# Row softmax: stores issued by Pool, DVE and ACT as loops over tiles

## The chip, the cores and the metric

The kernel runs on one core of a Trainium2 chip. The metric is the device time of one execution in microseconds (us). A core has several engines that run their own instruction streams: DVE (the vector engine), ACT (the scalar engine), POOL (GpSimd), PE (the matrix engine, unused here for arithmetic) and SP (which only issues transfers and waits). All transfers between HBM (the chip's memory) and SBUF (the core's working memory of 128 partitions) are carried out by 16 DMA engines, whichever engine issues them.

## The reference

A softmax over the last axis of a float32 array of 32 x 512 x 1024, with the input divided by a temperature of 0.5:

```
scaled = x / temperature
shifted = scaled - np.max(scaled, axis=-1, keepdims=True)
exp_x = np.exp(shifted)
return (exp_x / np.sum(exp_x, axis=-1, keepdims=True)).astype(np.float32)
```

There are 16,384 rows of 1,024 elements. 67.11 MB are read and 67.11 MB written.

## The kernel before, in words

The rows are cut into 16 tiles. A tile is 128 partitions x 8 rows x 1,024 elements, 4 MB; each partition holds eight neighbouring rows, so that its part of a tile is one piece of 32 KB in HBM and in SBUF. Six tile buffers (`BUFS = 6`) go round. All work is done in place in the tile.

A tile is worked on in two groups of four rows (`GROUP = 4`). The order is written out by hand, one step per group, and the program is fully unrolled: `maximum(g)` (DVE: the maxima of four rows in one `tensor_reduce`, L70, and the bias, which is minus twice the maximum, L73), `exponential(g)` (ACT: four activations of one row each, L79, which also sum up the row into `sums`), then `divide(g - 1)` (DVE: `reciprocal`, L91, and four multiplications of one row each by its reciprocal, L93) and `store(g - 1)`. DVE thus takes the maxima of the next group, which may lie in the next tile, before it divides the last one.

Loads are issued by SP (L61): six at the start, and then one each time a store has been issued. As a buffer is used anew, that load waits on SP until the store of the tile six before it has landed. Stores are issued by ACT (L101), one for a whole tile of 4 MB, after its second group has been divided; ACT waits for this division at that place in its own stream. `top`, `bias`, `sums` and `recip` are small buffers that go round in fours. The waits between the engines are set by the framework from what each instruction reads and writes.

Of the kernel before, what the change touches and what calls it, by code (L numbers as in the profile page):

```python
# [1 line left out]

# [4 lines left out]

TILES = [[8]] * 16  # L10
BUFS = 6

GROUP = 4


@with_exitstack
def kernel(
    ctx: ExitStack,
    tc: tile.TileContext,
    x: bass.AP,  # L20
    temperature: bass.AP,
    out: bass.AP,
):
    nc = tc.nc
    f32 = mybir.dt.float32
    scale = 1.0 / float(temperature)
    extreme = mybir.AluOpType.max if scale > 0 else mybir.AluOpType.min

    P = 128
    xf = x.flatten_outer_dims()  # L30
    of = out.flatten_outer_dims()
    n, d = xf.shape
    assert sum(sum(ks) for ks in TILES) * P == n

    data = ctx.enter_context(tc.tile_pool(name="data", bufs=BUFS))
    stats = ctx.enter_context(tc.tile_pool(name="stats", bufs=4))


    groups, first, r = [], [], 0
    for i, ks in enumerate(TILES):  # L40
        first.append(r)
        r += sum(ks)
        a = 0
        for k in ks:
            for b in range(0, k, GROUP):
                m = min(GROUP, k - b)
                groups.append((i, a + b, m, (a, k) if b + m == k else None))
            a += k

    def dram(t, i):  # L50
        k = sum(TILES[i])
        block = t[P * first[i] : P * (first[i] + k), :]
        return block.rearrange("(p k) d -> p k d", p=P, k=k)

    tiles, small = [], []

    def load():
        i = len(tiles)
        if i < len(TILES):
            xt = data.tile([P, sum(TILES[i]), d], f32, name="xt")  # L60
            nc.sync.dma_start(out=xt, in_=dram(xf, i))  # L61
            tiles.append(xt)

    def maximum(g):
        i, a, k, _ = groups[g]
        top, bias, sums, recip = (
            stats.tile([P, k], f32, name=name) for name in ("top", "bias", "sums", "recip")
        )
        small.append((bias, sums, recip))
        nc.vector.tensor_reduce(  # L70
            out=top, in_=tiles[i][:, a : a + k, :], axis=mybir.AxisListType.X, op=extreme
        )
        nc.vector.tensor_scalar_mul(bias, in0=top, scalar1=-scale)  # L73

    def exponential(g):
        i, a, k, _ = groups[g]
        bias, sums, _ = small[g]
        for b in range(k):
            nc.scalar.activation(  # L79
                tiles[i][:, a + b, :],  # L80
                tiles[i][:, a + b, :],
                mybir.ActivationFunctionType.Exp,
                bias=bias[:, b : b + 1],
                scale=scale,
                accum_out=sums[:, b : b + 1],
            )

    def divide(g):
        i, a, k, _ = groups[g]
        _, sums, recip = small[g]  # L90
        nc.vector.reciprocal(recip, sums)  # L91
        for b in range(k):
            nc.vector.tensor_scalar_mul(  # L93
                tiles[i][:, a + b, :], in0=tiles[i][:, a + b, :], scalar1=recip[:, b : b + 1]
            )

    def store(g):
        i, _, _, part = groups[g]
        if part:
            a, k = part  # L100
            nc.scalar.dma_start(out=dram(of, i)[:, a : a + k, :], in_=tiles[i][:, a : a + k, :])  # L101
            if a + k == sum(TILES[i]):
                load()

    with tc.manual_schedule():
        for _ in range(BUFS):
            load()
        for g in range(len(groups) + 1):  # L110
            if g < len(groups):
                maximum(g)
                exponential(g)
            if g > 0:
                divide(g - 1)
                store(g - 1)


# [1 line left out]
_INS = ['x', 'temperature']  # L120
_OUTS = [((32, 512, 1024), 'float32')]

_NUMBERS = {'temperature': 0.5}


# [26 lines left out]
```

## Time and profile before

| what | value |
|---|---|
| median of 10 runs | 318.04 us (317.73 to 318.38) |
| profiled execution, its own time | 317.98 us |
| its span in the profile | 316.1 us |
| DVE busy | 235.5 us, 74% of the span |
| ACT busy | 149.6 us, 47% |
| POOL busy | 0.2 us |
| moved by DMA | 134.25 MB, mean 425 GB/s over the span |
| first load issued | at 0.73 us |
| last store issued | at 302.47 us |

How to read it: the span goes from the first to the last instruction that the profile shows, and the time is 1.9 us longer than it. The profile's page names each engine's busy time, then the span in 40 equal slices with a digit for the busy share in tenths (9 is 90% or more), one line an engine and one for the mean of the 16 DMA engines. In the list of DMA queues q1 carries SP's loads, q10 ACT's stores and q14 the instructions that engines fetch; each line gives packets, MB and the share of the 16 engines' span that the packets took. In the groups of instructions, `out<-in` are the program's names and L93 is line 93 of the kernel. "Landing" is the time at which a transfer's last completion mark arrives.

### The profile page before, as it was taken

To read this page: it belongs to the slowest core of one execution; us is meant where nothing else is said; L and a number is where in the kernel's file an instruction comes from. 1 tells how busy PE (TensorE), PEld (TensorE's weight loads), DVE (VectorE), ACT (ScalarE), POOL (GpSimd) and SP (SyncE) were. 2 spreads that over 40 slices of the span, in tenths; PEclk is the share of its full clock that TensorE was granted. 3 is DMA by queue.
4 is the path that set the end of the run, shared out by engine and by line. 5 is a ranking of instruction groups with operands and counts; after the bars stand their busy time and mean duration, and the time that the engine had idled before them with its cause. 6 is when DMAs were issued, how large, how long until landed. Compare 5 with 4: busy or idle time off the path is not lost.

```text
span 316.1 us, 620 instructions
## 1 busy us (share of the span) xinstructions
DVE 235.5 (74%) x224; ACT 149.6 (47%) x257; POOL 0.2 (0%) x4
## 2 busy tenths in 40 slices
DVE  0399999999689494994949859497693976949720
ACT  0176666666526255361554605546064560645500
POOL 0000000000000000000000000000000000000000
DMA  8999999999999999999999999999999999999996
GB/s 332 423 440 427 386 448 431 431 437 419 452 419 448 415 456 406 456 406 456 406 456 419 444 424 440 444 419 452 411 452 412 456 406 456 406 456 411 452 406 274
DMA packets 4612, 134.25 MB, mean 425 GB/s; under 512 B 512, under 2 KB 512, under 8 KB 512
## 3 DMA queue, kind: packets, MB, share of 16 engines
q1 hardware_dynamic: 2304, 67.11, 49.6%
q10 hardware_dynamic: 2304, 67.11, 49.2%
q14 instruction: 4, 0.03, 0.0%
HBM read 67.11 MB, written 67.11 MB: 425 GB/s over the span
## 4 chain that ended last, share of the span: by engine, by line
DVE 72%; another core or an unknown queue 16%; DMA 4%; ACT 3%; issue 1%; DVEq 0%
DVE top L70 43%; DVE xt L93 27%; DMA xt<-in_x_dram 4%; ACT xt L79 3%; DVE recip L91 1%; DVE bias L73 1%; DVEq L147 0%
## 5 line engine op out<-in xcount | busy, mean ns | idle before, releaser
L79 ACT ACTIVATE xt<-xt,bias 128x1024 f32<-128x1024 f32 x128 | 145.4, 1137 | 137.0 <-DVE recip L91 119.6
L70 DVE TENSOR_REDUCE top<-xt 128x4 f32<-128x4096 f32 x32 | 141.3, 4416 | 62.7 <-DMA xt<-in_x_dram 62.7
L93 DVE TENSOR_SCALAR xt<-xt,recip 128x1024 f32<-128x1024 f32 x128 | 87.7, 749 | 1.1
L79 ACT ACTIVATION_READ_ACCUMULATOR xt<-xt,bias 128x1 f32 x128 | 23.8, 186 | 0.0
L79 ACT ACT_TABLE_LOAD x1 | 1.3, 1283 | 12.9 <-DMA xt<-in_x_dram 12.9
L91 DVE RECIPROCAL recip<-sums 128x4 f32<-128x4 f32 x32 | 5.5, 171 | 2.1 <-ACT xt L79 2.1
L73 DVE TENSOR_SCALAR bias<-top 128x4 f32<-128x4 f32 x32 | 5.4, 170 | 1.1
L133 POOL MEMSET const-uint8-127<- 128x1 uint8 x1 | 0.1, 102 | 0.0
L133 POOL MEMSET const-bfloat16-1.0<- 128x1 bf16 x1 | 0.1, 101 | 0.0
L133 POOL MEMSET const-float32-0.0<- 128x1 f32 x1 | 0.1, 98 | 0.2 <-issue 0.2
L133 POOL MEMSET const-float32-1.0<- 128x1 f32 x1 | 0.1, 98 | 0.0
## 6 DMA issues: line engine op xcount, KB each, us to landing
xt<-in_x_dram SPq DMA_DIRECT2D x16, 4096.0 KB, 51.2
out_dram<-xt ACTq DMA_DIRECT2D x16, 4096.0 KB, 38.1
```

The costliest lines, as they stand in the source:

```text
L70: nc.vector.tensor_reduce(out=top, in_=tiles[i][:, a : a + k, :], axis=mybir.AxisListType.X, op=extreme)
L73: nc.vector.tensor_scalar_mul(bias, in0=top, scalar1=-scale)
L79: nc.scalar.activation(tiles[i][:, a + b, :], tiles[i][:, a + b, :], mybir.ActivationFunctionType.Exp, bias=bias[:, b : b + 1], scale=scal ...
L91: nc.vector.reciprocal(recip, sums)
L93: nc.vector.tensor_scalar_mul(tiles[i][:, a + b, :], in0=tiles[i][:, a + b, :], scalar1=recip[:, b : b + 1])
L133: nc = _bacc.Bacc("TRN2", target_bir_lowering=False, num_devices=1)
```

## The change

The kernel is rewritten without the framework's scheduling, with semaphores of its own:

- The six buffers become one tile `ring` of 48 rows a partition; tile i lies in slot i % 6.
- Stores are issued by Pool, through its software descriptor queue, as soon as DVE has finished the tile's last group (it counts `scaled`). The last tile is stored in two halves of four rows (`LAST = [4, 4]`). Pool does nothing else. Each slot has its own semaphore for landed loads and for landed stores.
- PE turns the six semaphores of landed loads into one count, `ready`.
- DVE and ACT are loops over the 16 tiles, with the row's address computed from the loop's counter. A tile has groups of 4, 2 and 2 rows (`GROUPS`). DVE takes the maxima and biases of all three groups of a tile, and then divides its three groups; it no longer takes maxima of the next tile ahead of a division.
- ACT runs one tiny exponential ahead of its loop, so that its table is loaded before the first tile is there.
- SP issues all 16 loads, each from the seventh on behind a wait for the store of its slot, and at the end waits for the last stores.

The core of the diff:

```diff
-TILES = [[8]] * 16
-BUFS = 6
+SLOTS, ROWS = 6, 8
-GROUP = 4
+GROUPS = [4, 2, 2]
+LAST = [4, 4]
...
-            nc.scalar.dma_start(out=dram(of, i)[:, a : a + k, :], in_=tiles[i][:, a : a + k, :])
...
+    def take(engine, sem, count=1):
+        engine.wait_ge(sem, count).then_inc(sem, -count)
+
+    with tc.tile_critical(no_gpsimd_drain=True):
+        for i in range(tiles):
+            if i >= SLOTS:
+                nc.sync.wait_ge(stored[i % SLOTS], 16 * (i // SLOTS))
+            nc.sync.dma_start(out=slot(i), in_=dram(xf, i)).then_inc(loaded[i % SLOTS], 16)
+        for i in range(tiles):
+            nc.tensor.wait_ge(loaded[i % SLOTS], 16 * (i // SLOTS + 1)).then_inc(ready, 1)
+        for i in range(tiles - 1):
+            nc.gpsimd.wait_ge(scaled, len(groups) * (i + 1))
+            nc.gpsimd.dma_start(out=dram(of, i), in_=slot(i)).then_inc(stored[i % SLOTS], 16)
+        i = tiles - 1
+        for b, k in enumerate(LAST):
+            rows = slice(sum(LAST[:b]), sum(LAST[:b]) + k)
+            done = [a + m for a, m in groups].index(rows.stop) + 1
+            nc.gpsimd.wait_ge(scaled, len(groups) * i + done)
+            nc.gpsimd.dma_start(out=dram(of, i)[:, rows, :], in_=slot(i)[:, rows, :]).then_inc(
+                finished[b], 16
+            )
+
+        with nc.vector.Fori(0, tiles) as t:
+            first = t % SLOTS * ROWS
+            take(nc.vector, ready)
+            for a, k in groups:
+                nc.vector.tensor_reduce(
+                    out=top[:, a : a + k],
+                    in_=ring[:, bass.ds(first + a, k), :],
+                    axis=mybir.AxisListType.X,
+                    op=extreme,
+                ).then_inc(topped, 1)
+                take(nc.vector, topped)
+                nc.vector.tensor_scalar_mul(
+                    bias[:, a : a + k], in0=top[:, a : a + k], scalar1=-scale
+                ).then_inc(biased, k)
+            for a, k in groups:
+                take(nc.vector, summed, k)
+                nc.vector.reciprocal(
+                    recip[:, a : a + k], sums[:, a : a + k]
+                ).then_inc(inverted, 1)
+                take(nc.vector, inverted)
+                for b in range(a, a + k):
+                    row = ring[:, bass.ds(first + b, 1), :]
+                    ins = nc.vector.tensor_scalar_mul(row, in0=row, scalar1=recip[:, b : b + 1])
+                ins.then_inc(scaled, 1)
+
+        nc.scalar.activation(
+            warm, nc.const_aps.tensor(0.0, (P, 1)), mybir.ActivationFunctionType.Exp
+        )
+        with nc.scalar.Fori(0, tiles) as t:
+            first = t % SLOTS * ROWS
+            for b in range(ROWS):
+                row = ring[:, bass.ds(first + b, 1), :]
+                if b in of_group:
+                    take(nc.scalar, biased, of_group[b])
+                nc.scalar.activation(
+                    row,
+                    row,
+                    mybir.ActivationFunctionType.Exp,
+                    bias=bias[:, b : b + 1],
+                    scale=scale,
+                    accum_out=sums[:, b : b + 1],
+                ).then_inc(summed, 1)
+
+        for i in range(tiles - SLOTS, tiles - 1):
+            nc.sync.wait_ge(stored[i % SLOTS], 16 * (i // SLOTS + 1))
+        for sem in finished[:-1]:
+            nc.sync.wait_ge(sem, 16)
+    with tc.tile_critical(no_gpsimd_drain=True):
+        nc.sync.wait_ge(finished[-1], 16, synchronizes=[nc.sync.lower_ap(slot(tiles - 1))])
```

More of the change, by code (lines that the diff above doesn't have):

```diff
@@ L32 @@
     n, d = xf.shape
[L33 to L48, printed above, removed]
@@ L50, in dram @@
-    def dram(t, i):
[L51 to L67, printed above, removed]
-        )
[L69 to L100, printed above, removed]
-            nc.scalar.dma_start(out=dram(of, i)[:, a : a + k, :], in_=tiles[i][:, a : a + k, :])
[L102 to L116, printed above, removed]
+    tiles = n // (P * ROWS)
@@ new lines @@
+    assert tiles * P * ROWS == n and sum(GROUPS) == sum(LAST) == ROWS
+    groups = [(sum(GROUPS[:g]), k) for g, k in enumerate(GROUPS)]
+    of_group = dict(groups)
+    pool = ctx.enter_context(tc.tile_pool(name="data", bufs=1))
+    ring = pool.tile([P, SLOTS * ROWS, d], f32, name="ring")
+    top = pool.tile([P, ROWS], f32, name="top")
+    bias = pool.tile([P, ROWS], f32, name="bias")
+    sums = pool.tile([P, ROWS], f32, name="sums")
+    recip = pool.tile([P, ROWS], f32, name="recip")
+    warm = pool.tile([P, 1], f32, name="warm")
@@ new lines @@
+    loaded = [tc.alloc_semaphore(f"loaded{s}") for s in range(SLOTS)]
+    stored = [tc.alloc_semaphore(f"stored{s}") for s in range(SLOTS)]
+    finished = [tc.alloc_semaphore(f"finished{b}") for b in range(len(LAST))]
+    ready, topped, biased, summed, inverted, scaled = (
+        tc.alloc_semaphore(name)
+        for name in ("ready", "topped", "biased", "summed", "inverted", "scaled")
+    )
+    def dram(t, i):
+        return t[P * ROWS * i : P * ROWS * (i + 1), :].rearrange("(p k) d -> p k d", p=P, k=ROWS)
@@ new lines, in slot @@
+    def slot(i):
+        s = i % SLOTS
+        return ring[:, ROWS * s : ROWS * (s + 1), :]
+    def take(engine, sem, count=1):
[44 more added lines that the diff above has]
+            warm, nc.const_aps.tensor(0.0, (P, 1)), mybir.ActivationFunctionType.Exp
+        )
+        with nc.scalar.Fori(0, tiles) as t:
[16 more added lines that the diff above has]
+            nc.sync.wait_ge(sem, 16)
```

## The prediction

> **What bounds the kernel now.** I read four views in this order: the 40 slices of the page, the DMA queues, the costliest groups with the waits of DVE, and then the DMA queues of single stretches of the run.
>
> ```profile
> span 316.1 us, 620 instructions
> ...
> DVE 235.5 (74%) x224; ACT 149.6 (47%) x257; POOL 0.2 (0%) x4
> ...
> DMA  8999999999999999999999999999999999999996
> ...
> DMA packets 4612, 134.25 MB, mean 425 GB/s; under 512 B 512, under 2 KB 512, under 8 KB 512
> ...
> q1 hardware_dynamic: 2304, 67.11, 49.6%
> q10 hardware_dynamic: 2304, 67.11, 49.2%
> q14 instruction: 4, 0.03, 0.0%
> ```
>
> The 16 DMA engines show a 9 in every slice but the first and the last, while DVE works 74% and ACT 47% of the span. The two queues (q1 loads, q10 stores) together take 49.6 + 49.2 = 98.8% of 16 engines' time. So the kernel is bound by data movement, and DVE and ACT have room. A packet's size and price follow: 2,304 packets a queue are 2,048 of 32 KB (67.11 MB / 2,048) and 256 end markers; for q10, 0.492 x 16 x 316.1 / 2,048 = 1.215 us a packet (the markers are 9 ns each in the packet records; the records' usual 32 KB packet is 1,213 ns). One DMA engine has 4,096 / 16 = 256 data packets: 256 x 1.213 = 310.5 us of the 316.1. What is left over is under 6 us: the first packet starts at 1.7 us, and there is an end.
>
> ```profile
> L79 ACT ACTIVATE xt<-xt,bias 128x1024 f32<-128x1024 f32 x128 | 145.4, 1137 | 137.0 <-DVE recip L91 119.6
> L70 DVE TENSOR_REDUCE top<-xt 128x4 f32<-128x4096 f32 x32 | 141.3, 4416 | 62.7 <-DMA xt<-in_x_dram 62.7
> L93 DVE TENSOR_SCALAR xt<-xt,recip 128x1024 f32<-128x1024 f32 x128 | 87.7, 749 | 1.1
> ```
>
> In each row stand the busy time, the mean of one, and the idle time before it with what ended it. All the idle time of the maxima (L70) is time in which they wait for a load: 62.7 us, from 84 us on about 4.5 us in every tile. The compute engines are therefore behind DMA, not ahead of it. The chain of waits names DVE for 72% of its length, but in the windows DMA moves 433 GB/s from 68 to 282 us with no gap, so that chain is not what sets the time.
>
> The end decides what is left. These are the DMA queues of 313.0 to 316.1 us, and below them those of 64 to 68 us:
>
> ```profile
> DMA packets 18, 0.07 MB, mean 21 GB/s; under 512 B 16, under 2 KB 16, under 8 KB 16
> ...
> q10 hardware_dynamic: 18, 0.07, 5.2%
> ```
>
> ```profile
> q1 hardware_dynamic: 30, 0.52, 32.2%
> q14 instruction: 2, 0.02, 1.0%
> ```
>
> At 313.0 us sixteen end markers are still to come but only two data packets (0.07 MB): two of the 16 DMA engines are late. In the packet records 13 engines write their last marker at 313.06 to 313.33 us, the three others at 313.68, 314.41 and 314.90; the kernel ends when the last one is there. What made them late can be seen: q14 carries four instruction packets of 8 KB inside the span, two at 64.9 us and one each at 181.9 and 240.2 us. Each takes 309 ns, and the data packet beside it is stretched by 535, 535, 268 and 533 ns. One such meeting thus costs its engine 0.58 to 0.84 us. One of 0.58, two of 0.84, and one of 0.84 on an engine that began 0.39 us after the first give lags of 0.58, 1.68 and 1.23 us behind 313.1 us, which fit 313.68, 314.90 and 314.41. This assignment to engines is mine; the records don't name the engine.
>
> [...]
>
> **The change, part by part.**
> 1. *Loops.* DVE's program has 33 rows in place of 224 computing ones, ACT's 26 in place of 257[...]. If all of it is there before the first load, the four q14 packets in the span go. The last marker then comes with the bulk and the late starter, 313.33 to 313.45, in place of 314.90: **-1.5 us** (bounds -1.6 and 0; zero if fetches remain).
> 2. *Order within a tile.* Now DVE does all maxima of a tile and then all divisions: maxima 4.42 + 2 x 2.21 = 8.8, three biases and three reciprocals 6 x 0.17 = 1.0, divisions 2 x 2.74 = 5.5, together about 15.4 us with its waits, and ACT's 8 x 1.13 = 9.1 us run beside it (first group 4.6 to 9.1 us, last 13.7, after which two divisions remain: 15.6 us from landing to the last division). A tile's DMA takes 256 packets over 16 engines, 16 x 1.213 = 19.4 us for load and store. So 3.8 us a tile are free. [...] If divisions fell to the rate of a maximum (1.1 us) a tile took 18.6 us, still inside. Cost: nothing, hidden by the queued DMA.
> 3. *When a store starts.* Before, store i waited behind the first maximum of tile i+1 (load 14 landed at 263.4, its store was issued at 290.2). Now it goes about 16 us after landing, the first at 12.8 + 15.6 = 28.4 us plus Pool's delay, for 32.5. Slots come free earlier, loads are issued earlier; with DMA always busy this gains nothing.
> 4. *Pool in place of ACT.* 17 issues leave ACT's queue (16 x 0.34 us, where ACT idles 137 us anyway) for a queue with nothing behind it but the next store. [...] Cover: queued loads, and at the end about 1.75 tiles of earlier stores. That number: loads ran alone until about 29 us, 27 us at 9.7 us a tile, and so stay 2.75 tiles ahead if the queues then share evenly. When load 15 lands, 1.75 x 9.7 = 17 us of stores lie ahead of store 15, [...]. Cost: nothing[...].
> 5. *The software ring's packets.* Unknown. If every 32 KB packet stays whole, [...] = **+0.2 us**. Bounds: none below[...], above see the second rival.
> 6. *Start and end.* SP passes one more branch and a no-op before its first load (0.73 us now), the end has one more round of sequencer waits; the ones now at the end run from 315.4 to 316.1 us. **+0.25 us** (0 to 0.9). The last store in halves adds 16 markers, 9 ns an engine: nothing. PE's 16 waits and SP's waits for stores lie behind loads that are queued two tiles deep.
>
> Sum: 317.98 (the profiled execution: span 316.1 and 1.9 outside it) - 1.5 + 0.2 + 0.25 = 316.9. The median of the ten is 318.04, 0.06 more: **317.0 us**. This kernel's measurement can tell about 0.2%, 0.64 us, from no change.
>
> **Rivals.**
> - *The fetches stay or the savings are eaten*[...]: 317.4 to 318.7. For it: the loops' back branches are in no trace[...]. Against it: programs this short. If every turn of a loop fetched anew, 16 turns would put dozens of packets of 0.8 us on the engines, and the time would be over 325; I give that little.
> - *Slower: the software ring's store packets cost more.* Place: the 128 store packets on the slowest engine. By the records a packet has a fixed part: 4 x 309 - 1,213 = 23 ns for three more packets, 7.7 ns each. Stores cut to 16 KB cost 128 x 7.7 = 1.0 us, to 8 KB 3.0, to 4 KB 6.9. [...] From about 10 ns a packet the gain is gone; from 15 ns it is slower. Middle value 321. Against it: [...] total traffic is the same.
> - *Slower: a hole before the last store.* If the stores' ring is served ahead of the loads', no backlog builds up: load 15 lands with 0.8 tiles of store 14 left, 8 us[...]
>
> **Chances.** The forecast (316.2 to 317.4, its own range to 317.9 with the bounds) 0.50; no difference 0.21; the ring's price 0.19, the hole 0.06, repeated fetches 0.04. Faster by over 0.2% 0.50, within 0.21, slower 0.29. The range goes from 315.9 (all bounds at their best, and an earlier start) to 322.0, which leaves out the 4 KB packets, the hole and the fetches.
>
> **What would show it.** Right: no q14 packet between the first load and the last store; in the window of the last 3 us all 16 engines' last data packets within 0.5 us; a software queue with 2,048 packets of 32 KB (and some in halves) and a share near 49%. Step 2: maxima that wait for loads as now, about 4 us a tile. Wrong: a store queue whose share exceeds 50%, more or smaller packets, a digit under 9 in the slices before the last, or the first load later than 1.5 us.

## The result, and the profile after

The changed kernel takes 324.03 us (median of 9 runs, 322.18 to 325.49) against 318.01 us for the kernel before (30 runs beside it): a ratio of 1.018, 95% interval 1.0166 to 1.0193. It is slower by 6.0 us, where 317.0 us was forecast with 322.0 us as the upper end. The profiled execution took 324.52 us, 6.54 us more than that of before.

The first view is the page of the changed kernel: the busy times, the DMA row of the 40 slices, and the DMA queues (packets, MB, share of 16 engines' span). The lines answer to those shown of before.

```profile
span 322.8 us, 1209 instructions
...
DVE 244.5 (76%) x272; ACT 148.1 (46%) x258; POOL 9.6 (3%) x21
...
DMA  8999999999999999999999999999999999999993
...
DMA packets 4752, 134.22 MB, mean 416 GB/s; under 512 B 528, under 2 KB 528, under 8 KB 528
...
q1 hardware_dynamic: 2304, 67.11, 49.7%
q0 software_dynamic: 2448, 67.11, 48.3%
```

The DMA engines are still busy in every slice but the first and the last, so no hole has opened. Yet they moved 416 GB/s in place of 425. The traffic is the same but for the instruction packets: q14, which stood at 4 packets before, is gone. The software queue holds 2,448 packets: 1,920 of 32 KB and 256 of 16 KB by the packet records, and 272 end marks.

The groups of the changed kernel show that DVE and ACT still wait for data:

```profile
L92 DVE TENSOR_REDUCE top<-ring 128x2 f32 (+1 forms) x48 | 143.8, 2996 | 48.6 <-DVEq L66 48.6
L110 DVE TENSOR_SCALAR ring<-ring,recip x128 | 89.1, 749 | 7.2 <-DVEq L66 2.0
...
L78 POOL DMA_DIRECT2D out_dram<-ring x15 | 8.1, 540 | 279.8 <-DVE ring L110 279.8
```

A row's division takes 749 ns, as before. The maxima idle 48.6 us ahead of their 48 instructions; that is their wait for the next tile. Pool spends 0.54 us on an issue and waits 279.8 us for DVE.

So the lost time is inside the transfers. To find it, I read windows of equal stretches of both kernels. The columns are: stretch, its length, busy time and instructions of DVE, ACT and POOL, the PE clock, DMA share, and GB/s. A packet counts in the stretch in which it starts, so a share can pass 1. First the changed kernel, then the kernel before:

```profile
128.00:131.00 3.00, 0.00 (x0) 0.00 (x0) 0.39 (x1) 1.00 1.03 437
131.00:135.00 4.00, 3.53 (x1) 0.00 (x0) 0.00 (x0) 1.00 0.97 352
135.00:148.00 13.00, 11.78 (x17) 9.16 (x16) 0.02 (x1) 1.00 1.00 434
208.00:213.00 5.00, 2.03 (x1) 0.00 (x0) 0.32 (x1) 1.00 1.04 400
247.00:253.00 6.00, 2.56 (x2) 0.00 (x0) 0.53 (x1) 1.00 1.00 388
```

```profile
131.00:135.00 4.00, 3.93 (x8) 3.55 (x7) 0.00 (x0) 1.00 0.95 410
...
208.00:213.00 5.00, 4.93 (x8) 3.52 (x7) 0.00 (x0) 1.00 1.02 439
...
247.00:253.00 6.00, 5.93 (x8) 4.28 (x7) 0.00 (x0) 1.00 1.01 437
```

Most of the run has the old rate (437, 434). In short stretches the DMA engines are just as busy and move 9 to 14% less: 352 against 410, 400 against 439, 388 against 437 GB/s. A packet in such a stretch takes longer. In the packet records a normal packet of 32 KB takes 1,213 ns; in these stretches some take 1.3 to 2.3 us. Of this added time 89% lies in the 4 us after the first of the 16 end marks of a store (130.9 us for the stretch from 131, 209.0 for the one from 208, 248.2 for the one from 247), while loads run beside it. After 40 us, the packets of 32 KB take 3.96 us more per engine than at 1,213 ns each; before, this sum was 0.21 us. It is the firmer figure: in a stretch of 4 us, one packet more or less on each of the 16 engines is 131 GB/s.

The engines are not hit alike, so the end spreads. The DMA queues of the changed kernel from 313.0 to 316.1 us:

```profile
DMA packets 88, 1.23 MB, mean 396 GB/s; under 512 B 13, under 2 KB 13, under 8 KB 13
...
q0 software_dynamic: 88, 1.23, 92.8%
```

Here the kernel before had 18 packets and 0.07 MB left to move; the changed one still moves 1.23 MB in this window. Its 16 last marks come between 315.88 and 320.85 us; before, 13 were there by 313.33 and the last at 314.90.

Where this begins is in the timelines. The first line is the changed kernel's first store, the second that of before (in brackets the idle time ahead of it and what ended it):

```profile
30.03 0.67 POOL L78 DMA_DIRECT2D out_dram<-ring  x1 [29.59 <-DVE ring L110]
```

```profile
32.53 0.37 ACTq L101 DMA_DIRECT2D out_dram<-xt  x1
```

The first store is issued 2.5 us earlier, as forecast. From then on the load queue and the store queue take turns: by the changed kernel's packet records, from 100 to 107 us, 12 to 14 packets of one queue start in a turn of 1.21 us, and 12 to 14 of the other in the next. In the changed kernel store 0 ends 2.5 us behind load 3 (first end marks 53.1 and 50.6 us); at load 7 and store 4 it is 2.5 us again (130.9 and 128.4). Before, it was 7.3 us (55.1 and 47.9), and 7.3 again at the same later pair. In these two kernels the moment of the first store thus fixes a **distance of ends** that stays as it is, until the loads end, within 0.1 us. Whether this is what costs the time is the question of the experiments.

### The profile page after: what moved, and what is told of

It is laid out like the page before. It is cut to its first block, busy times and chain, and to the rows that moved or that the text cites. A ratio compares the mean times of both kernels' runs of the same rounds, so it can differ in the third digit from the quotient of the medians.

```text
span 322.8 us, 1209 instructions
## 1 busy us (share of the span) xinstructions
DVE 244.5 (76%) x272; ACT 148.1 (46%) x258; POOL 9.6 (3%) x21
## 3 DMA queue, kind: packets, MB, share of 16 engines
q1 hardware_dynamic: 2304, 67.11, 49.7%
q0 software_dynamic: 2448, 67.11, 48.3%
## 5 line engine op out<-in xcount | busy, mean ns | idle before, releaser
L123 ACT ACTIVATE ring<-ring,bias x128 | 145.1, 1135 | 156.4 <-ACTq L66 156.4
L92 DVE TENSOR_REDUCE top<-ring 128x2 f32 (+1 forms) x48 | 143.8, 2996 | 48.6 <-DVEq L66 48.6
L110 DVE TENSOR_SCALAR ring<-ring,recip x128 | 89.1, 749 | 7.2 <-DVEq L66 2.0
L123 ACT ACTIVATION_READ_ACCUMULATOR ring<-ring,bias 128x1 f32 x128 | 23.9, 187 | 0.0
L78 POOL DMA_DIRECT2D out_dram<-ring x15 | 8.1, 540 | 279.8 <-DVE ring L110 279.8
L99 DVE TENSOR_SCALAR bias<-top 128x2 f32<-128x2 f32 (+1 forms) x48 | 8.1, 170 | 7.2
L104 DVE RECIPROCAL recip<-sums 128x2 f32<-128x2 f32 (+1 forms) x48 | 7.9, 164 | 0.0
L84 POOL DMA_DIRECT2D out_dram<-ring x2 | 1.3, 664 | 18.6 <-DVE ring L110 18.6
```

The source lines that it names most:

```text
L78: nc.gpsimd.dma_start(out=dram(of, i), in_=slot(i)).then_inc(stored[i % SLOTS], 16)
L84: nc.gpsimd.dma_start(out=dram(of, i)[:, rows, :], in_=slot(i)[:, rows, :]).then_inc(finished[b], 16)
L92: nc.vector.tensor_reduce(out=top[:, a : a + k], in_=ring[:, bass.ds(first + a, k), :], axis=mybir.AxisListType.X, op=extreme,).then_inc(t ...
L99: nc.vector.tensor_scalar_mul(bias[:, a : a + k], in0=top[:, a : a + k], scalar1=-scale).then_inc(biased, k)
L104: nc.vector.reciprocal(recip[:, a : a + k], sums[:, a : a + k]).then_inc(inverted, 1)
L110: ins = nc.vector.tensor_scalar_mul(row, in0=row, scalar1=recip[:, b : b + 1])
```

## The experiments

Six theories stand in the expectations below under letters:

- **A**: the software queue's store packets are dearer in themselves.
- **B**: the loops and the new way of running DVE and ACT cost time whatever queue stores.
- **C**: DVE's divisions hold Pool's stores up, or make them dearer.
- **D**: the two queues lose their step, because of the moment and the manner in which the first store begins (in one form: the engines begin it in unequal turns). Its later form, **D'**, says that only the distance between the end of a load and the end of a store counts.
- **E**: the order of work (a tile's maxima, then its divisions) does it, apart from the moment of the first store.
- **G**, **G'**: a later first store is better as such, whatever the distance.

Where a number of packets, marks or excess is given below, it is from the packet records, and "excess" is what the packets of 32 KB take over 1,213 ns each after 40 us, as a mean per engine. These figures are of each kernel's profiled execution. The distance is that between the first end mark of the first store and of the load nearest to it.

### One part alone

**Pool's stores alone.** The kernel before, with one word changed:

```diff
-            nc.scalar.dma_start(out=dram(of, i)[:, a : a + k, :], in_=tiles[i][:, a : a + k, :])
+            nc.gpsimd.dma_start(out=dram(of, i)[:, a : a + k, :], in_=tiles[i][:, a : a + k, :])
```

> The kernel before with one edit: its stores are issued by Pool in place of ACT; program, order and fetches stay. Theory A (the software queue: each time it passes from one store to the next while loads run beside it, the 16 DMA engines lose unequal time): 321.5 to 325 us, load packets stretched right after each store's end marks, end marks of one store drifting 4 to 6 us apart. Theory B (loops and the order of work in a tile cost it): 317.5 to 318.5 us, marks within 2 us.

Measured: 318.15 us, ratio 1.0001 (0.9993 to 1.001). From its page:

```profile
span 316.4 us, 639 instructions
...
q0 software_dynamic: 2304, 67.11, 49.1%
q14 instruction: 4, 0.03, 0.0%
```

All of the stores go over the software queue and the kernel is as fast as before. Its share, 49.1%, is that of the hardware queue before (49.2%). Store 0 ends 9.7 us behind load 3; the excess is 0.12 us. Theory A falls.

**The loops' order with ACT's stores.** The changed kernel with ACT written out, so that it can issue a tile's store after the tile's exponentials; Pool stores nothing:

```diff
-            nc.gpsimd.wait_ge(scaled, len(groups) * (i + 1))
-            nc.gpsimd.dma_start(out=dram(of, i), in_=slot(i)).then_inc(stored[i % SLOTS], 16)
...
+                nc.scalar.wait_ge(scaled, len(groups) * (i + 1))
+                nc.scalar.dma_start(out=dram(of, i), in_=slot(i)).then_inc(stored[i % SLOTS], 16)
```

> The changed kernel with its stores issued by ACT through its hardware queue; to that end ACT's program is written out in place of its loop, and DVE's loop and the order stay. Theory A: 316.3 to 317.8 us, all end marks of the last store within 2 us (ACT's program still fetches two packets). Theory B: 322 to 325 us.

Measured: 337.85 us (four runs: 331.58, and three from 337.83 to 338.24), against 318.12. The loss is there without the software queue, and larger. Store 0 goes at 29.9 us and ends 1.2 us behind load 3; from the next pair on the distance is 2.3 to 2.5 us. Here single engines fall behind until a whole tile waits for them. Load 7 has its first mark at 128.5 and its last at 140.0 us. In the windows of its end (columns as above) the other engines stand idle twice:

```profile
295.00:305.00 10.00, 7.74 (x13) 6.15 (x12) 0.00 (x0) 1.00 0.42 180
...
314.00:320.00 6.00, 5.55 (x9) 6.00 (x11) 0.00 (x0) 1.00 0.13 56
```

This speaks for B, D or E, and again against A.

**Stores in two DMAs**, each over 64 partitions (the waits for `stored` then count to 32 in place of 16):

```diff
-            nc.gpsimd.dma_start(out=dram(of, i), in_=slot(i)).then_inc(stored[i % SLOTS], 16)
+            for h in (slice(0, 64), slice(64, 128)):
+                nc.gpsimd.dma_start(out=dram(of, i)[h], in_=slot(i)[h]).then_inc(
+                    stored[i % SLOTS], 16
+                )
```

> The changed kernel with 15 of its stores cut into two of 64 partitions each: the same 32 KB packets, twice as many boundaries between stores. Theory A with a price per boundary: the loss of some 4 to 5 us over a clean run doubles, 327 to 330 us. If the price is per packet of the software queue: 323 to 325 us, no change.

Measured: 374.19 us (358.33 to 382.78), far outside what either theory expected. In the profiled execution, the one of 358.33 us, the excess is 25 us per engine, on loads and stores. The first store ends 4.9 us ahead of a load, and the later ones fall anywhere between the loads' ends. The edit changes the size of a DMA, the number of ends and their distance together, so it tells no theory from another. Why it is so much slower stays open, and what is said of distances below holds for stores of 4 MB alone.

**No divisions.** This kernel leaves the divisions out, so it writes the exponentials undivided:

```diff
-                for b in range(a, a + k):
-                    row = ring[:, bass.ds(first + b, 1), :]
-                    ins = nc.vector.tensor_scalar_mul(row, in0=row, scalar1=recip[:, b : b + 1])
-                ins.then_inc(scaled, 1)
+                nc.vector.tensor_scalar_mul(
+                    top[:, a : a + k], in0=recip[:, a : a + k], scalar1=1.0
+                ).then_inc(scaled, 1)
```

> The changed kernel without the divisions of rows: in each group DVE multiplies the few reciprocals by one instead, so the output is the exponentials undivided[...]. Theory C [...]: 316.5 to 318.5 us. Theory A: 322 to 325 us, load packets stretched as in the changed kernel.

Measured: 317.77 us (317.6 to 319.89), ratio 0.9998 (0.9988 to 1.0009). The loss is gone, with Pool's stores, the loops and the order of groups all kept. So B falls. But the edit does two things: it takes the divisions away, and it moves the first store from 30.0 to 28.7 us. With that, store 0 and load 3 end together (both 51.7 us). C and D both explain it, and a later pair below tells them apart.

### The moment of the first store alone

**A memset on Pool ahead of its first store**, of 512, 1,024, 2,048 and then 3,500 elements. Nothing else is changed, and only the first store can be late by it:

```diff
+    idle = pool.tile([P, 512], f32, name="idle")
...
         for i in range(tiles - 1):
             nc.gpsimd.wait_ge(scaled, len(groups) * (i + 1))
+            if i == 0:
+                nc.gpsimd.memset(idle, 0.0)
```

> The changed kernel; Pool writes zeros over 512 elements a partition of a spare buffer ahead of its first store, which so goes later by some half a microsecond to a microsecond; nothing else. Theory D (lost step: the first store's packets arrive while the 16 DMA engines pass a packet's end one after the other within 0.6 us, at 31.5 to 32.1 us, so that some take a store packet a turn before the others; from then on some engines load while others store, and lose time where transfers change): the time depends on where the first store falls, 316.2 to 317.5 us if it falls clear of that spread, 321 to 326 if not; 0.6 us may or may not be enough. Theory E (the order of work in a tile, with its divisions in one run, costs it): 322 to 325 us whatever the delay.

> As the run before it, with 1,024 elements, a delay of about 1 to 2 us. Theory D: 316.2 to 317.5 us if the first packets of the first store start on all engines in one turn, with end marks of a store within 1 us; else above 321. Theory E: 322 to 325 us.

> As before, with 2,048 elements, a delay of about 2 to 4 us. Theory D: at least one of these three delays gives 316.2 to 317.5 us. Theory E: 322 to 325 us for all three.

> The changed kernel with Pool's zeros over 3,500 elements ahead of its first store, issued at about 33 us, so that a store ends some 8 to 10 us after a load. Theory D: no stretched packets after the first store's start; 317.2 to 318.5 us, the changed kernel's loss gone. Theory E: 322 to 325 us.

| memset | first store, us | distance, us | excess, us | time, us | ratio (95%) |
|---|---|---|---|---|---|
| none (the changed kernel) | 30.03 | 2.5 | 3.96 | 324.03 | 1.018 (1.0166 to 1.0193) |
| 512 | 30.29 | 3.6 | 2.69 | 322.95 | 1.0143 (1.0122 to 1.0163) |
| 1,024 | 30.86 | 4.1 | 0.27 | 319.95 | 1.005 (1.0036 to 1.0064) |
| 2,048 | 31.54 | 5.7 | 0.11 | 319.07 | 1.0026 (1.0016 to 1.0036) |
| 3,500 | 32.88 | 8.3 | 0.10 | 319.02 | 1.0032 (1.002 to 1.0043) |

The pieces of the last one, in its timeline:

```profile
29.92 3.02 POOL L80 MEMSET idle<- 128x3500 f32 x1 [29.48 <-DVE ring L113]
32.88 0.67 POOL L81 DMA_DIRECT2D out_dram<-ring  x1
```

1.5 us of waiting at 30 us, once, give back 5 us at the end. This is the experiment that carries most: nothing but the moment of one store differs. It leaves the order, the loops, the queue and the divisions as they were, so B, E and the plain form of C can't explain it. What remains above the kernel before, 0.3%, is not excess; it is looked at below. It is also why none of the four came down to the times that theory D named (316.2 to 317.5 us, and 317.2 to 318.5 us for the last).

**The kernel before with an early first store.** The reverse: the old kernel, its order changed for tile 0 only, so that it is divided and stored before tile 1's maxima.

```diff
         for g in range(len(groups) + 1):
+            if g == 2:
+                divide(1)
+                store(1)
             if g < len(groups):
...
-            if g > 0:
+            if g > 0 and g != 2:
                 divide(g - 1)
```

> The kernel before, with one edit: the second group of tile 0 is divided and tile 0 stored ahead of the maxima of tile 1, so its first store is issued at about 29.6 us in place of 32.5; hardware queue, unrolled program and the order of every later tile stay. Theory D (only the moment of the first store against the end of load 2, at 31.4 to 31.8 us, matters): the ends of stores come 1 to 3 us after the ends of loads, load packets are stretched there, 321 to 335 us. Theory E (the changed kernel's order of work, or its queue): 317.5 to 318.5 us.

Measured: 323.86 us, ratio 1.0187 (1.0171 to 1.0202). The first store goes at 30.1 us, from ACT; the distance is 3.2 us at the first pair and 2.4 to 2.6 us from the third on, and the excess is 4.42 us. From its page:

```profile
span 321.9 us, 620 instructions
...
DMA packets 4612, 134.25 MB, mean 417 GB/s; under 512 B 512, under 2 KB 512, under 8 KB 512
...
q10 hardware_dynamic: 2304, 67.11, 48.4%
q14 instruction: 4, 0.03, 0.0%
```

The whole loss of the changed kernel stands here in the old one, with no loop, no software queue, the same instructions and the same 134.25 MB: 417 GB/s against 425.

**No divisions, and late.** The kernel without divisions, with a memset of 1,536 ahead of its first store:

```diff
+            if i == 0:
+                nc.gpsimd.memset(idle, 0.0)
```

> The changed kernel without the divisions of rows (as in the run that took 317.8 us; the output is the exponentials undivided), and with Pool's zeros over 1,536 elements ahead of the first store, which then goes at about 30.1 us as in the changed kernel. Theory D: 321 to 326 us, with stretched load packets, though no division runs. Theory E or C (the divisions do it): 317.5 to 318.5 us.

Measured: 324.57 us, ratio 1.02 (1.0179 to 1.022). The timelines of the two kernels without divisions show the first store 1.1 us apart (without the memset, then with it), and the windows show what follows from it (same order):

```profile
28.75 0.67 POOL L78 DMA_DIRECT2D out_dram<-ring  x1 [28.30 <-DVE top L108]
```

```profile
29.86 0.67 POOL L81 DMA_DIRECT2D out_dram<-ring  x1
```

```profile
208.00:213.00 5.00, 4.85 (x3) 0.10 (x1) 0.00 (x0) 1.00 1.03 446
...
247.00:253.00 6.00, 5.85 (x3) 1.30 (x3) 0.00 (x0) 1.00 1.01 437
```

```profile
208.00:213.00 5.00, 1.97 (x1) 0.00 (x0) 0.00 (x0) 1.00 1.04 380
...
247.00:253.00 6.00, 1.88 (x1) 0.00 (x0) 0.00 (x0) 1.00 0.97 366
```

446 and 437 GB/s become 380 and 366. No division runs in either kernel. The distance is 0 in the first and 2.4 us in the second. So C falls, and so does G: later is worse here. All 16 engines began this kernel's first store within one packet (34.8 to 35.4 us), so the unequal turns in D are not needed either.

### From a hardware queue, at other moments

**Spare exponentials ahead of ACT's first store.** Two, and then five, exponentials of a zeroed buffer in the kernel with ACT's stores were to make its first store late:

```diff
+                for c in range(2 if i == 0 else 0):
+                    nc.scalar.activation(
+                        spare[:, c, :], idle, mybir.ActivationFunctionType.Exp
+                    )
```

> The kernel with DVE's loop and stores from ACT's hardware queue (337.9 us), its first store put behind two spare exponentials of 1,024 elements, some 2.2 us later. Theory D: 316.2 to 318 us if that clears the spread, and well above 322 if not. A theory in which the hardware queue with this order of work is slow by itself: 330 to 338 us.

> DVE's loop with stores from ACT's hardware queue, five spare exponentials ahead of the first store, issued at about 35 us. Theory D: 316.6 to 317.8 us, since half of the fetches is gone and the hardware queue ends sooner than the software one. If the first store's moment were not what decides: 325 us or more, as with two exponentials.

Measured: 325.26 us with two (324.24 to 334.02), ratio 1.021 (1.019 to 1.0229), and 337.06 with five, 1.0605 (1.057 to 1.0639). Both missed their aim: the store did not become late. It left at 29.8 and 29.9 us, while the first spare exponential was running. So they are two more looks at an early store from a hardware queue (distance 1.7 us at the first pair of both, 2.4 to 2.6 us from the next one on; the profiled execution of the first was its longest, 334.02 us), and tell nothing about a late one.

**The same with a semaphore.** Three exponentials, and a wait for the count that the last one raises:

```diff
+                if i == 0:
+                    for c in range(3):
+                        nc.scalar.activation(
+                            spare[:, c, :], idle, mybir.ActivationFunctionType.Exp
+                        ).then_inc(blank, 1)
+                    nc.scalar.wait_ge(blank, 4)
```

> DVE's loop with stores from ACT's hardware queue, as in the runs of 337.9, 325.3 and 337.1 us; this time the first store waits on a semaphore until three spare exponentials are done, so that it is really issued at about 33 us (in the earlier two it still went at 29.9). Theory D' (a store that ends within some 1 to 4 us after a load costs time, whatever queue): stores end 7 us or more after loads, no stretched packets, 316.8 to 318.2 us. If the hardware queue with this order of work were slow by itself: 325 us or more.

Measured: 318.44 us, ratio 1.0013 (1.0007 to 1.002). The timelines, first of the run with five that did not hold the store and then of this one:

```profile
29.88 1.06 ACT L113 ACTIVATE spare<-idle 128x1024 bf16<-128x1024 f32 x1 [2.21 <-DVE ring L100]
29.89 0.38 ACTq L116 DMA_DIRECT2D out_dram<-ring  x1
30.84 3.88 ACT L113 ACTIVATE spare<-idle 128x1024 bf16<-128x1024 f32 x4
```

```profile
29.84 2.95 ACT L114 ACTIVATE spare<-idle 128x1024 bf16<-128x1024 f32 x3 [2.21 <-DVE ring L100]
32.82 0.37 ACTq L118 DMA_DIRECT2D out_dram<-ring  x1
```

From 29.9 to 32.8 us, and the kernel with ACT's stores falls from 337 to 318.4 us; distance 7.3 us, excess 0.13. At this distance the hardware queue loses nothing either. The 318.44 us are a little above the 318.2 that were expected at most.

**Is later simply better?** The changed kernel, its first store held until DVE is a given number of groups on in tile 1; the aim was to reach the near distance again, one load later.

```diff
+                nc.vector.wait_ge(inverted, 1).then_inc(turn, 1)
...
+            if i == 0:
+                nc.gpsimd.wait_ge(turn, len(groups) + 1)
```

> The changed kernel with its first store held until the first reciprocals of tile 1 are done, at about 39.8 us, 10 us later than it was and again some 2 us ahead of a load's end (load 3's, at about 41.7). Theory D': the ends of stores come 2 to 3 us after those of loads again, 321 to 326 us. Theory G (the later the first store, the better, whatever the ends): 317.5 to 319.2 us, as with 33 us.

> The changed kernel with its first store held until the last maximum of tile 1 is taken, aimed at 39.5 to 39.9 us, 1.8 to 2.2 us ahead of load 3's end; the run before it, aimed there too, was issued only at 40.8 us and its stores ended 5.7 us after loads. Theory D' (only the distance counts): if it is issued there, stores end 2 to 3.5 us after loads, load packets are stretched, 321 to 326 us, though the store is 10 us later than in the changed kernel. Theory G' (a first store after 30 us is late enough): 318.4 to 319.2 us.

Both missed the aim: the first store went at 40.8 and 40.6 us, with store 0 5.8 and 4.8 us behind load 4. They took 318.92 (1.0028, 1.0017 to 1.0039) and 318.85 us (1.0027, 1.0018 to 1.0036); once the first store has begun, their excess is 0.1 us. In the second the count is taken at the maxima (`topped`) in place of the reciprocals. With one group fewer there and a memset of 2,304 the aim was met:

```diff
+            if i == 0:
+                nc.gpsimd.wait_ge(turn, 2 * len(groups) - 1)
+                nc.gpsimd.memset(idle, 0.0)
```

> The changed kernel with its first store held until the second maximum of tile 1 and then Pool's zeros over 2,304 elements, aimed at 39.7 us, 2 us ahead of load 3's end (the run aimed there before was issued at 40.6 us, its stores ended 4.9 us after loads, and it took 318.85 us). Theory D': if issued at 39.4 to 39.9 us, stores end 1 to 3.5 us after loads, load packets are stretched, 321 to 326 us. Theory G' (a first store after 30 us is late enough): 318.4 to 319.2 us.

Measured: 323.5 us, ratio 1.016 (1.0114 to 1.0206). The first store goes at 39.4 us and ends 2.4 us behind load 4; the excess is 4.55 us, of which 0.65 us is the start of the first store. Windows of the same stretch, first of this kernel and then of the one at 40.8 us:

```profile
218.50:223.00 4.50, 2.39 (x1) 0.00 (x0) 0.00 (x0) 1.00 1.05 379
```

```profile
218.50:223.00 4.50, 4.20 (x5) 2.77 (x5) 0.00 (x0) 1.00 1.05 451
```

**Is early bad?** Tile 0's store in two halves, the first when its first four rows are done (the waits for slot 0 count these 16 marks more):

```diff
+        for b in range(2):
+            rows = slice(4 * b, 4 * b + 4)
+            nc.gpsimd.wait_ge(scaled, (1, len(groups))[b])
+            nc.gpsimd.dma_start(out=dram(of, 0)[:, rows, :], in_=slot(0)[:, rows, :]).then_inc(
+                stored[0], 16
+            )
```

> The changed kernel with its first tile stored in two halves, as its last one is: the first goes at about 26.5 us, 3.5 us earlier than before. Theory D': the ends of stores fall far from those of loads (a first store at 26.5 us is over 5 us ahead of load 2's end): no stretched packets, 317.3 to 319.2 us. Theory G (later is better): 324 us or more.

Measured: 318.42 us, ratio 1.0014 (1.0007 to 1.002). The first half goes at 26.9 us, earlier than in any other kernel here, and stores end 3.2 us ahead of loads, from the store of the second half on (59.6 and 62.8 us), where over 5 us had been expected; excess 0.07. So it matters which of the two ends first: some 3 us behind a load there is a loss, 3.2 us ahead of one there is none. An earlier store is fast and a later one is slow (39.4 us), so it is not the moment as such: G' falls too.

### All of them by distance

| kernel | store queue | first store, us | distance, us | from the next store on, us | excess, us | time, us |
|---|---|---|---|---|---|---|
| first tile in halves | software | 26.9 | -3.2 | -3.2 | 0.07 | 318.42 |
| no divisions | software | 28.7 | 0 | 0 | 0.12 | 317.77 |
| ACT's stores in the loops' order | hardware | 29.9 | 1.2 | 2.3 to 2.5 | 5.58 | 337.85 |
| five exponentials, not held | hardware | 29.9 | 1.7 | 2.4 to 2.5 | 4.50 | 337.06 |
| two exponentials, not held | hardware | 29.8 | 1.7 | 2.4 to 2.6 | 5.73 | 325.26 |
| changed kernel | software | 30.0 | 2.5 | 2.4 to 2.5 | 3.96 | 324.03 |
| no divisions, late | software | 29.9 | 2.4 | 2.4 to 2.5 | 4.53 | 324.57 |
| first store at 39.4 us | software | 39.4 | 2.4 | 2.4 to 2.6 | 4.55 | 323.50 |
| before, first store early | hardware | 30.1 | 3.2 | 2.4 to 2.9 | 4.42 | 323.86 |
| memset of 512 | software | 30.3 | 3.6 | 3.0 to 3.4 | 2.69 | 322.95 |
| memset of 1,024 | software | 30.9 | 4.1 | 4.4 to 4.8 | 0.27 | 319.95 |
| held to 40.6 us | software | 40.6 | 4.8 | 4.8 | 0.79 | 318.85 |
| memset of 2,048 | software | 31.5 | 5.7 | 5.6 | 0.11 | 319.07 |
| held to 40.8 us | software | 40.8 | 5.8 | 5.7 to 5.8 | 1.04 | 318.92 |
| before | hardware | 32.5 | 7.3 | 7.3 | 0.21 | 318.01 |
| ACT's store held | hardware | 32.8 | 7.3 | 7.3 | 0.13 | 318.44 |
| memset of 3,500 | software | 32.9 | 8.3 | 8.3 | 0.10 | 319.02 |
| Pool's stores alone | software | 33.1 | 9.7 | 9.7 | 0.12 | 318.15 |

(In the three runs whose first store goes after 39 us, the excess holds the start of that store too, which costs 0.5 to 0.9 us an engine in every row and lies ahead of 40 us in the others. For the first tile in halves the distance is that of the second half. The next stores are counted as long as loads run beside them.)

The loss follows the distance, on both queues, in both orders of work, with and without divisions, at 30 us and at 39 us. It is there in every run whose later pairs lie 2.3 to 3.4 us apart, nearly gone in the one that moves from 4.1 to 4.8 us, and absent at 0, at -3.2 and from 4.8 us on. That is shown. The runs that began at 1.2 and 1.7 us went over to about 2.5 us at the next pair, so no run shows what a lasting distance of 1.2 us does. Nor does the distance give the size of the loss in time: at about the same 2.5 us, ACT's stores in the loops' order cost 7 to 20 us and the others 5.6 to 6.6.

The packet records tell more of what the distance is. All 16 engines, or most of them, do the same at the same time: in one turn of about 1.21 us they carry a load packet, in the next a store packet. Where a DMA ends, in all the rows below but the last, its queue misses a turn and the other has two in a row. L is a turn with load packets, S one with store packets, and the star is the turn in which the end marks of that pair's load (after S) or store (after L) stand:

```
changed kernel, from 66.7 us          S L S S* L L* S          loss
first store at 39.4 us, from 57.0     S L S S* L L* S          loss
held to 40.6 us, from 58.1            S S* L S L L* S          none
ACT's store held, from 66.4           S S* L S L S L L* S      none
first tile in halves, from 59.4       L L* S S* L              none (13 of the 16 engines)
no divisions                          S L S L S L ...          none (both ends in one turn)
```

The loss is there in runs where the doubled load turn follows at once on the doubled store turn. With one L and one S between them it is gone, and in the other order (L L S S) too. Most of the stretched packets stand in and after the second L. The order alone doesn't bring the loss about at once: in the second row (9 of the 16 engines, the others one turn later) no packet is stretched at this first pair yet; it begins at the next pair, 19 us on, with the same order. Why these packets take longer is not shown. In the two rows with a loss the ends of a load and a store lie 2.4 to 2.6 us apart, and this distance also fixes which parts of two tiles are moved at one time. No run here separates the two; it stays open.

No version beat the kernel before. The one with a lower median, without divisions, leaves work out and can't be told from it; Pool's stores alone are equal to it, and the best complete ones with the new order (ACT's store held, and the first tile in halves) are 0.13 and 0.14% above it.

## Why the prediction was wrong

**What bounds the kernel: right.** DMA is still at 9 in every slice but the first and the last; DVE and ACT wait.

**Step 3, when a store starts: this is the step that failed.** It had the moment of issue nearly right (28.4 us plus Pool's delay; the division ended at 29.7 and the store was issued at 30.0), and then said of stores and loads that start earlier, "with DMA always busy this gains nothing", and gave the edit no bound. A gain was excluded rightly, but so was a loss, and nothing in the profile excluded one. DMA always busy says how long the engines work, not how much they move: with a 9 in all slices but the first and the last in both kernels, it was 425 GB/s and then 416. The kernel before had shown one distance, 7.3 us, and its 1,213 ns a packet held for that distance. The working order carried this number over to a run in which the queues stand otherwise. It cost 6.96 us on the slowest DMA engine (last mark 320.85 us, against 313.89 in the kernel without divisions, where the two queues end together), 3.84 us on the mean one (excess 3.96 less 0.12).

**Step 1, loops: right in kind.** q14 is gone, and with it the late engines that it made. In the kernel without divisions, which has the loops and no loss, the last mark comes at 313.89 us; before it came at 314.90, from loads that began 0.21 us sooner. That is -1.2 us on an equal start, for the -1.5 forecast. No loop fetched anything in the span, so the rival of repeated fetches is out as well.

**Step 2, order within a tile: right.** Tile 14 takes 16.2 us from its first maximum to the end of its last division (271.34 to 287.56 us) (15.6 forecast), under the 19.4 us of its transfers, and costs nothing by itself. What it does is to move the first store. As forecast, the maxima still wait for loads, those of tiles 14 and 15 for 4.2 and 3.7 us.

**Step 4, Pool in place of ACT: right.** No hole opened ahead of the last store. Pool issues 0.3 us after a division ends, in 0.53 us; while divisions run beside it the issue of the last tile's first half takes 0.80 us. One size was off without harm: the first packet of the first store starts at 34.9 us, 5.2 us after the division's end, so that loads ran alone for 3.4 tiles in place of the 2.75 that the author had estimated. It is not Pool that takes this time: before, 4.45 us passed from ACT's issue to the first packet (32.53 and 36.98 us).

**Step 5, the software queue's packets: right.** Packets stay whole (32 KB, and 16 KB for the halves). The 0.2 us that the sum adds for them was the author's estimate, which no trace showed. In the kernel with Pool's stores alone 95% of the store packets take 1,213 ns, and its time can't be told from that of before. The rival with dearer store packets named the right sign and a near time (321) for a cause that is not there. Nor does the software queue by itself spread the engines' ends: with Pool's stores alone the last marks of all 16 lie within 1.5 us (313.09 to 314.56), before within 1.8, and in the kernel without divisions, which fetches no instructions, within 0.8 (313.13 to 313.89). The records don't name the engines.

**Step 6, start and end: too small, inside its bounds.** The first load is issued at 0.94 us in place of 0.73. (ACT's table load of 1.28 us, which stood at 12.88 us, now stands at 0.91 us, ahead of the first tile.) From the last mark to the end of the span it takes 1.90 us in place of 1.20. Outside the span it is 0.11 us less (324.52 - 322.75 against 317.98 - 316.10). Together 0.80 us, for 0.25 taken. This alone put the forecast of 317.0 out of reach: without the loss, the kernels of this form took 317.77 to 319.07 us, which is the first rival (the savings are eaten) or a little above it. Those at about 319.0 have a further part, a single late engine: with the memset of 3,500 fifteen engines end by 313.90 us and one at 315.21. Why it is late stays open. Six engines began that kernel's first store a turn late, but in the kernel held to 40.6 us all 16 began within 0.42 us, and one still ended at 314.96, the others by 313.74.

The difference of the two profiled executions adds up: the last mark +5.95 us (0.21 start, -1.22 fetches, and +6.96 loss, which is the rest), the end +0.70, outside the span -0.11, in all 6.54.

**Its signs.** The vanished q14 packets and a store share near 49% (48.3%) came as named for a right forecast; last packets within 0.5 us of each other did not (last marks over 5 us). None of the signs named for a wrong one came: they all look at the queue, the slices and the first load, and none at the price of a load packet.

## What to carry to other kernels

When two queues keep the DMA engines full, "always busy" need not be "always at the same rate" (here packets of 32 KB took 3.96 us more per engine than at 1,213 ns each, with DMA at 9 in all slices but two): read GB/s beside the busy share in short windows, and look for packets longer than the usual one. An edit that moves the first transfer of a queue can set how the two queues stand for the whole run (here 2.5 us apart in place of 7.3, from a store 2.5 us earlier), so bound it from below and above even where everything is hidden, and try the kernel with that one transfer moved by a microsecond or two. Where a change that makes nothing on the path slower still costs time, move the moment back alone, before blaming the new queue or the new loop.

## What was not expected of the hardware

- Loads and stores of 4 MB that take turns packet by packet lose, in these runs, 5 to 6.6 us of 318 from a software queue, and 6 to 20 from a hardware queue, when stores end 2.3 to 3.4 us behind loads over the run; at 0, 3.2 us ahead, or 4.8 us and more throughout, packets are hardly stretched (excess of 0.1 us once the stores have begun), and the times are at most 1.1 us above that of before. In the changed kernel a first store that comes 1.5 us later (31.54 us) takes the loss away: excess 0.11 in place of 3.96 us, time 319.07 in place of 324.03.
- A DMA issued by ACT was not held by the activations ahead of it in ACT's program: with five of them before it, it left at 29.89 us, 0.01 us after the first had begun. Only a wait on their semaphore held it (32.82 us).
- The DMA engines don't share such a loss evenly: in the changed kernel the last marks of the 16 spread over 5 us. In the loops' order with ACT's stores load 7 came 11.5 us after its first mark (128.5 to 140.0 us), and the whole tile had to wait for it.
